# An adaLN transformer block on one core: a first modulation group of two k-tiles, an earlier silu(c) and x, and partition sums as matmuls with ones

## The chip, the core and the metric

The kernel runs on one core of one Trainium2 chip. The metric is the device time of one execution in microseconds (us). The engines are TensorE (PE; its weight loads are listed as PEld), VectorE (DVE), ScalarE (ACT), GpSimd (POOL) and SyncE (SP), which issues most DMAs. Each works through its own list of instructions in order.

## What is computed

One transformer block on 256 tokens with model width 2048, all in float32. A conditioning vector c gives six vectors of width 2048, which shift, scale and gate the two halves of the block:

```python
mod = silu(c) @ w_ada + b_ada
shift_m, scale_m, gate_m, shift_f, scale_f, gate_f = split(mod, 6)
h = modulate(rms_norm(x, pre_norm_mix), shift_m, scale_m)   # h * (1 + scale) + shift
q_n, k_c, v_c, k_s, v_s, k_w, v_w, g_n, q_m, k_m, v_m = split(h @ w_in)
o = concat(nsa_mixer(...), moba_mixer(...)) @ w_o
x = x + gate_m * rms_norm(o, post_norm_mix)
h = modulate(rms_norm(x, pre_norm_ffn), shift_f, scale_f)
x = x + gate_f * rms_norm(square(relu(h @ w_up)) @ w_down, post_norm_ffn)
```

w_ada is 2048 x 12288, w_in 2048 x 5656, w_up 2048 x 8192 and w_down 8192 x 2048. Every weight is read once.

## The kernel before

**Tiles.** The 256 tokens are two token tiles of 128; the width of 2048 is 16 k-tiles of 128. A product of float32 operands is made of three matmuls: both operands are split into a rounded high part and a low part, and `products` (L495) issues hi x hi (L496), hi x lo (L497) and lo x hi (L498). So each tile of weights needs an ACT cast for the high part (L491) and a DVE subtraction for the low part (L492) before PE can use it.

**The modulation vectors** are sums over 2048 rows of w_ada, with silu(c) as coefficients. They are not made on PE: `gemv_units` (L280) loads rows of w_ada and DVE multiplies each k-tile by its column of silu(c) (`csil`) and adds it to an accumulator of 128 partitions (L305 for the first, L310 for the others). What is left is a sum over the partitions: `reduce` (L338) transposes the accumulator on PE (L345), sums it up along the free axis on DVE (L347), and lets POOL add the bias (L351) and multiply by the norm gain (L353). Then `main` of `mod_units` (L356) scales and shifts the transposed, normalized x on ACT (L372), and splits it (L375 on ACT, L376 on DVE).

**Groups and passes.** M_MODS = (4, 4, 4, 4) says that the first half's modulation is made for four k-tiles at a time; the groups are named modm0, modm4, modm8 and modm12. The in-projection follows in passes: all six blocks of columns (kv, kw, qn, qm, km, vm; 1024 columns each, kw 536) for k-tiles 0 to 3, then all for 4 to 7, then qm and km for 8 to 11, and so on. Within a block the k-tiles are summed up in four PSUM banks. At the end of a block ACT copies the banks out in the first pass (L571), and in every later pass DVE adds them to what is there (L573). In F_MODS the second half's groups are modf0 to modf12.

**Order.** The program is a list of units (a load, a preparation, a main part), which `Stream.run` (L104) writes out in order. Loads run ahead as far as five raw buffers reach, preparations up to four units (AHEAD) and five split weight tiles (WBUFS). `spread` (L134) sets where in a pass the units of the next modulation group stand (L935 to L945): the group modm4 is made during the pass over k-tiles 0 to 3, and so on. A scheduler then settles the order on each engine; what stands under `tc.high_priority()` it brings forward. All large loads go through SP's queue.

**The start.** The six small DMAs of constants are on ACT's queue (L213 to L218); POOL builds an identity and the attention masks; the loads of modm0 begin, x follows (`x_units`, L513), is squared and summed on ACT (L525), scaled on DVE (L529) and transposed on PE (L274). In-projection products begin once modm0 has been summed up, and its k-tiles are modulated and split.

Of the kernel before, what the change touches and what calls it, by code (L numbers as in the profile page):

```python
# [12 lines left out]
F32 = mybir.dt.float32  # L13
F32R = mybir.dt.float32r
# [61 lines left out]
class Stream:  # L76
    """Emits units in order; loads and preparations run ahead as far as the buffers reach."""
# [56 lines left out]
def spread(base, extra, first, last):  # L134
    """The units of base with the groups in extra placed between positions first and last."""
# [17 lines left out]
def tile_adaln_block(ctx: ExitStack, tc: tile.TileContext, x, c, w_ada, b_ada, g_pm, g_qm, w_in,  # L153
# [28 lines left out]
    # Constants  # L182
    ident = cp.tile([P, P], F32, name="ident")
    make_identity(nc, ident)
    onesr = cp.tile([P, P], F32R, name="onesr")
    nc.scalar.activation(onesr, ident, AF.Identity, bias=1.0, scale=0.0)
    identb = cp.tile([P, P], BF16, name="identb")
    nc.vector.tensor_copy(identb, ident)
    sel4 = cp.tile([P, 32], F32, name="sel4")
    nc.vector.tensor_add(sel4, ident[:, 0:32], ident[:, 32:64])  # L190
    nc.vector.tensor_add(sel4, sel4, ident[:, 64:96])
    nc.vector.tensor_add(sel4, sel4, ident[:, 96:128])
    mhalf = cp.tile([P, 1], F32, name="mhalf")
    nc.gpsimd.memset(mhalf, -0.5)

    maskf = accp.tile([P, NT, NCMP + T], F32, tag="acc", name="maskf")
    nc.gpsimd.memset(maskf, 0.0)
    for t in range(NT):
        nc.gpsimd.affine_select(
            out=maskf[:, t, 0:NCMP], in_=maskf[:, t, 0:NCMP], compare_op=ALU.is_ge, fill=NEG,  # L200
            base=t * P - (CLEN - 1), pattern=[[-CSTR, NCMP]], channel_multiplier=1)
        nc.gpsimd.affine_select(
            out=maskf[:, t, NCMP:], in_=maskf[:, t, NCMP:], compare_op=ALU.is_ge, fill=NEG,
            base=t * P, pattern=[[-1, T]], channel_multiplier=1)
# [1055 lines left out]
```

## Time and profile before

| | |
|---|---|
| time, median of 3 runs | 1200.63 us (1200.17 to 1202.42) |
| span of the profiled execution, first to last instruction | 1199.2 us |
| PE busy | 1140.5 us, 95% |
| DVE busy | 908.5 us, 76% |
| ACT busy | 602.2 us, 50% |
| POOL busy | 32.7 us, 3% |
| mean DMA rate | 260 GB/s |

The page has no time of its own for the profiled execution but its span; the median of the runs is 1.4 us above it. Busy time is the time in which an instruction of the engine was running. A table of stretches gives, for each stretch of the span, the busy time of every engine with the number of instructions in parentheses, the granted clock of TensorE as a share of 2.4 GHz, the busy share of the DMA engines and the rate.

### The profile page before, as it was taken

What the parts mean: (1) busy time and instruction counts of PE and PEld (TensorE: products, weight loads), DVE (VectorE), ACT (ScalarE), POOL (GpSimd) and SP (SyncE); (2) the same over time, 40 slices, a digit from 0 to 9 for tenths busy, and PEclk for the clock granted to TensorE, in tenths of its full rate; (3) what the DMA queues carried; (4) which work ended last, traced back from release to release, by engine and by line L of the source; (5) the groups of instructions that cost most, each with busy time, mean ns of one, the idle gap of its engine ahead of it and who ended that gap; (6) DMA issues with size and microseconds to landing.
All of it is one profiled execution on the core that took longest, in us unless ns stands there. A gap on an engine that the chain in (4) does not pass through costs nothing.

```text
span 1199.2 us, 14451 instructions
## 1 busy us (share of the span) xinstructions
PE 1140.5 (95%) x5429; PEld 935.9 (78%) x5429; DVE 908.5 (76%) x1086; ACT 602.2 (50%) x922; POOL 32.7 (3%) x38
## 2 busy tenths in 40 slices
PE   2599998999999999999999999999999999999997
PEld 1477886878778887888888788888888888888885
DVE  6877999879998897876988986757666666665564
ACT  3446343436756666665343344767544444444441
POOL 1000001000000031000000000000000000000000
PEclk9699999999999999999999999999999999999999
DMA  9898989886766695997867875555677767775541
GB/s 334 311 392 277 361 307 336 261 293 246 273 223 233 246 356 178 360 333 276 315 250 279 315 266 193 176 176 187 215 258 268 259 253 274 253 278 178 207 142 70
DMA packets 88249, 312.02 MB, mean 260 GB/s; under 512 B 6051, under 2 KB 6515, under 8 KB 75251
## 3 DMA queue, kind: packets, MB, share of 16 engines
q1 hardware_dynamic: 87876, 311.01, 72.6%
q8 instruction: 42, 0.69, 0.2%
q14 instruction: 27, 0.21, 0.0%
q10 hardware_dynamic: 304, 0.11, 0.0%
HBM read 308.99 MB, written 2.10 MB: 259 GB/s over the span
## 4 chain that ended last, share of the span: by engine, by line
PE 81%; DVE 9%; issue 3%; DMA 3%; ACT 2%; POOL 1%; DVEq 0%; POOLq 0%; ACTq 0%
PE dps L498 9%; PE dps L496 9%; PE dps L497 9%; PE up L496 9%; PE up L498 9%; PE up L497 9%; DVE modm L310 3%; PE wo L496 2%; PE wo L498 2%; PE wo L497 2%; PE ft L1083 1%; PE in_vm L497 1%; PE in_vm L498 1%; PE in_vm L496 1%; PE in_kv L496 1%
## 5 line engine op out<-in xcount | busy, mean ns | idle before, releaser
L310 DVE SCALAR_TENSOR_TENSOR modf<-modf,csil,modf 128x1024 f32<-128x1024 f32 x60 | 76.7, 1278 | 9.2 <-DMA modf<-in_w_ada_dram 9.1
L310 DVE SCALAR_TENSOR_TENSOR modm<-modm,csil,modm 128x1024 f32<-128x1024 f32 x60 | 76.8, 1280 | 0.9
L1099 DVE TENSOR_TENSOR facc<-up,facc 128x512 f32<-128x512 f32 x96 | 61.5, 683 | 18.7 <-PE up L498 18.7
L310 DVE SCALAR_TENSOR_TENSOR gatef<-gatef,csil,gatef 128x1024 f32<-128x1024 f32 x32 | 40.6, 1278 | 1.3 <-DMA gatef<-in_w_ada_dram 1.3
L310 DVE SCALAR_TENSOR_TENSOR gatem<-gatem,csil,gatem 128x1024 f32<-128x1024 f32 x32 | 40.2, 1273 | 0.0
L1139 DVE TENSOR_TENSOR flo<-facc,fhi 128x512 fp32r<-128x512 f32 x32 | 21.7, 684 | 2.0 <-ACT fhi L1138 2.0
L1138 ACT CAST fhi<-facc 128x512 fp32r<-128x512 f32 x32 | 19.7, 624 | 5.3 <-PE up L497 1.9
L1101 ACT ACTIVATE facc<-facc 128x512 f32<-128x512 f32 x32 | 18.4, 624 | 2.8 <-DVE facc L1099 2.8
L1097 ACT COPY facc<-up 128x512 f32<-128x512 f32 x32 | 17.8, 594 | 1.6 <-PE up L498 1.0
L492 DVE TENSOR_TENSOR up_13lo<-up,up_13hi 128x1024 fp32r<-128x1024 f32 x8 | 9.8, 1226 | 11.5 <-ACT up_13hi L491 11.5
L492 DVE TENSOR_TENSOR up_14lo<-up,up_14hi 128x1024 fp32r<-128x1024 f32 x8 | 9.8, 1224 | 11.1 <-ACT up_14hi L491 11.1
L345 PE MATMUL modm0t<-ident,modm 128*128 128x128 f32 x8 | 1.9, 424 | 17.0 <-DVE modm L310 17.0
L1088 ACT ACTIVATE facc<-ft 128x512 f32<-128x512 f32 x32 | 17.2, 588 | 0.4 <-PE ft L1083 0.2
L1083 PE MATMUL ft<-ident,facc 128*128 128x128 f32 x128 | 16.8, 273 | 0.0
L1083 PEld LDWEIGHTS ft<-ident,facc 128*128 128x128 f32 x128 | 14.7, 140 | 2.6 <-ACT facc L1088 0.5
L492 DVE TENSOR_TENSOR up_0lo<-up,up_0hi 128x1024 fp32r<-128x1024 f32 x8 | 9.8, 1223 | 7.7 <-ACT up_0hi L491 7.7
L491 ACT CAST up_7hi<-up 128x1024 fp32r<-128x1024 f32 x8 | 8.4, 1056 | 14.3 <-PE up L498 14.3
L491 ACT CAST up_11hi<-up 128x1024 fp32r<-128x1024 f32 x8 | 8.4, 1055 | 14.2 <-PE up L498 14.2
L351 POOL TENSOR_TENSOR modf0red<-modf0red,cola 128x8 f32<-128x8 f32 x1 | 9.0, 8993 | 227.3 <-ACT wo_15hi L491 227.3
L491 ACT CAST up_10hi<-up 128x1024 fp32r<-128x1024 f32 x8 | 8.4, 1056 | 13.3 <-PE up L498 13.3
L491 ACT CAST up_6hi<-up 128x1024 fp32r<-128x1024 f32 x8 | 8.4, 1055 | 13.3 <-PE up L498 13.3
L345 PEld LDWEIGHTS modm0t<-ident,modm 128*128 128x128 f32 x8 | 1.6, 224 | 17.2 <-ACT in_kv_1hi L491 17.2
(2340 smaller groups left out, 4020.2 us busy)
## 6 DMA issues: line engine op xcount, KB each, us to landing
up<-in_w_up_dram SPq DMA_DIRECT2D x64, 1024.0 KB, 6.6
dn<-in_w_down_dram SPq DMA_DIRECT2D x64, 1024.0 KB, 4.9
modm<-in_w_ada_dram SPq DMA_DIRECT2D x64, 512.0 KB, 6.5
modf<-in_w_ada_dram SPq DMA_DIRECT2D x64, 512.0 KB, 5.9
gatem<-in_w_ada_dram SPq DMA_DIRECT2D x16, 1024.0 KB, 4.9
wo<-in_w_o_dram SPq DMA_DIRECT2D x16, 1024.0 KB, 5.3
gatef<-in_w_ada_dram SPq DMA_DIRECT2D x16, 1024.0 KB, 4.8
in_kv<-in_w_in_dram SPq DMA_DIRECT2D x8, 1024.0 KB, 7.3
```

Of the source, the lines that this page charges most:

```text
L310: nc.vector.scalar_tensor_tensor(part, w[:, j:j + step], csil[:, k:k + 1], part, ALU.mult, ALU.add)
L491: nc.scalar.copy(hi[:, 0:n], src)
L492: nc.vector.tensor_sub(lo[:, 0:n], src, hi[:, 0:n].bitcast(F32))
L496: nc.tensor.matmul(o, shi, whi, start=first, stop=False)
L497: nc.tensor.matmul(o, shi, wlo, start=False, stop=False)
L498: nc.tensor.matmul(o, slo, whi, start=False, stop=last)
L1083: nc.tensor.transpose(b[:, (2 * i + t) * P:(2 * i + t + 1) * P], f[:, t, (2 * j + i) * P:(2 * j + i + 1) * P], ident)
L1097: nc.scalar.copy(dst, b)
L1099: nc.vector.tensor_add(dst, b, dst)
L1101: nc.scalar.activation(dst, dst, AF.Relu)
L1138: nc.scalar.copy(hi, f)
L1139: nc.vector.tensor_sub(lo, f, hi.bitcast(F32))
```

## The change

- The first half's modulation is made in groups of 2, 2, 4, 4 and 4 k-tiles; the in-projection gets a pass over k-tiles 0 and 1 and a pass over k-tiles 2 and 3 in place of the one over 0 to 3. A group of two k-tiles is loaded four k-tiles of w_ada at a time (four DMAs of 256 KB each), where a group of four takes two at a time (two DMAs of 512 KB).
- The positions at which the units of the groups stand in the passes are new.
- silu(c) is computed at the start with high priority, straight from PSUM; the DMAs of x get high priority too, so that they stand ahead of those of w_ada. Masks, two identities, `sel4` and the positions' transposes move from the start into `late_constants`, in the pass over k-tiles 2 and 3; two small DMAs move from ACT's queue to SP's.
- `reduce` sums over the partitions with matmuls: each 128 x 128 piece of the accumulator is the stationary operand and a column of ones the moving one, so that one PSUM column per piece is the result. Bias and gain are applied by DVE.
- In the first group, odd k-tiles are modulated on DVE.

```diff
-M_MODS = (4, 4, 4, 4)
+M_MODS = (2, 2, 4, 4, 4)
...
+    one = cp.tile([P, 1], F32, name="one")
+    nc.gpsimd.memset(one, 1.0)
...
+    with tc.high_priority():
+        pc = bank("pconst0")
+        nc.tensor.transpose(pc[:, 0:16], stagec, ident[0:16, 0:16])
+        sigmoid_parts(csil, pc[:, 0:KD])
+        nc.vector.reciprocal(csil, csil)
+        nc.vector.tensor_mul(csil, csil, pc[:, 0:KD])
...
     def late_constants():
         nc.sync.dma_start(rp, rope)
         nc.sync.dma_start(w2[:, 0, :], ck_w2[0])
         nc.sync.dma_start(w2[:, 1, :], cv_w2[0])
+        nc.sync.dma_start(stageb[0:32, :], ck_pos[0])
+        nc.sync.dma_start(stageb[32:64, :], cv_pos[0])
+        nc.scalar.activation(onesr, ident, AF.Identity, bias=1.0, scale=0.0)
+        nc.scalar.copy(identb, ident)
+        mask_constants()
+        nc.vector.tensor_add(sel4, ident[:, 0:32], ident[:, 32:64])
+        nc.vector.tensor_add(sel4, sel4, ident[:, 64:96])
+        nc.vector.tensor_add(sel4, sel4, ident[:, 96:128])
+        pb = bank("pconst")
+        nc.tensor.transpose(pb[:, 0:64], stageb, ident[0:64, 0:64])
+        nc.scalar.copy(colb, pb[:, 0:64])
...
-        units = gemv_units(name, base + k0 * P, W, True, 2 if W <= 512 else 1, acc, first)
+        units = gemv_units(name, base + k0 * P, W, True, min(1024 // W, 4), acc, first)
...
-                for i0 in range(0, 2 * nk, 4):
-                    n = min(4, 2 * nk - i0)
-                    b = bank(f"{name}t{i0}")
-                    for i in range(n):
-                        nc.tensor.transpose(b[:, i * P:(i + 1) * P],
-                                            acc.t[:, (i0 + i) * P:(i0 + i + 1) * P], ident)
-                    nc.vector.tensor_reduce(red[:, i0:i0 + n],
-                                            b[:, 0:n * P].rearrange("p (k q) -> p k q", k=n),
-                                            axis=AX.X, op=ALU.add)
+                b = bank(f"{name}t")
+                for i in range(2 * nk):
+                    nc.tensor.matmul(b[:, i:i + 1], acc.t[:, i * P:(i + 1) * P], one,
+                                     start=True, stop=True)
                 ks = slice(k0, k0 + nk)
-                nc.gpsimd.tensor_add(red.rearrange("p (s k) -> p s k", s=2),
-                                     red.rearrange("p (s k) -> p s k", s=2), bias[:, :, ks])
-                nc.gpsimd.tensor_mul(red[:, nk:], red[:, nk:], gcol[:, ks])
+                nc.vector.tensor_add(red.rearrange("p (s k) -> p s k", s=2),
+                                     b[:, 0:2 * nk].rearrange("p (s k) -> p s k", s=2),
+                                     bias[:, :, ks])
+                nc.vector.tensor_mul(red[:, nk:], red[:, nk:], gcol[:, ks])
...
-                    modulate(xv[:, k % 2, :], xv[:, k % 2, :], *of(k))
+                    if tag == "m" and k0 == 0 and k % 2:
+                        shift, scale = of(k)
+                        nc.vector.tensor_scalar(xv[:, k % 2, :], xv[:, k % 2, :], scale, shift,
+                                                ALU.mult, ALU.add)
+                    else:
+                        modulate(xv[:, k % 2, :], xv[:, k % 2, :], *of(k))
...
-            for h, v in enumerate(st["x"]):
-                nc.sync.dma_start(v, x[t * P:(t + 1) * P, h * 1024:(h + 1) * 1024])
+            with tc.high_priority():
+                for h, v in enumerate(st["x"]):
+                    nc.sync.dma_start(v, x[t * P:(t + 1) * P, h * 1024:(h + 1) * 1024])
...
-    base = flat(in_pass(blocks, 0, 4))
-    m0 = [u for grp in mods[0] for u in grp]
-    stream.add(m0[:8] + [early(u) for u in base[:2]] + m0[8:])
-    base += [Unit(None, late_constants)]
-    stream.add(spread(base, mods[1], 6, len(base) - 7))
+    base = flat(in_pass(blocks, 0, 2))
+    m0 = flat(mods[0])
+    stream.add(m0[:3] + [early(base[0])] + m0[3:])
+    stream.add(spread(base, mods[1], 1, len(base) - 3))
+    base = flat(in_pass(blocks, 2, 4))
+    base.insert(2, Unit(None, late_constants))
+    stream.add(spread(base, mods[2], 0, len(base) - 2))
     base = flat(in_pass(blocks, 4, 8))
-    stream.add(spread(base, mods[2], 2, len(base) - 5))
+    stream.add(spread(base, mods[3], 0, len(base) - 5))
...
-    stream.add(spread(base, mods[3][:-1], 0, len(base)))
-    stream.add(mods[3][-1])
+    stream.add(spread(base, mods[4][:-1], 0, len(base)))
+    stream.add(mods[4][-1])
```

## Rows read from the trace of the kernel before

**Rows 1.** The page: busy us of each engine, share of span, instructions.

```profile
PE 1140.5 (95%) x5429; PEld 935.9 (78%) x5429; DVE 908.5 (76%) x1086; ACT 602.2 (50%) x922; POOL 32.7 (3%) x38
```

**Rows 2.** Stretches: us, busy of PE, PEld, DVE, ACT, POOL, PEclk, DMA share, GB/s.

```profile
15.00:37.30 22.30, 5.07 (x31) 4.36 (x29) 21.36 (x20) 6.88 (x18) 1.59 (x1) 0.72 1.04 393
37.30:112.80 75.50, 66.67 (x305) 54.41 (x306) 58.35 (x56) 41.59 (x61) 4.27 (x4) 0.92 0.88 323
112.80:175.60 62.80, 61.76 (x297) 51.43 (x296) 58.66 (x66) 26.70 (x32) 2.18 (x2) 1.00 0.90 325
175.60:200.70 25.10, 22.04 (x93) 16.91 (x92) 24.99 (x25) 6.57 (x7) 0.00 (x0) 1.00 0.96 357
200.70:226.40 25.70, 24.20 (x110) 19.52 (x109) 21.26 (x26) 11.02 (x16) 4.01 (x3) 1.00 0.74 253
...
500.00:780.00 280.00, 279.42 (x1261) 231.43 (x1260) 223.48 (x235) 139.91 (x168) 2.97 (x7) 1.00 0.76 271
```

**Rows 3.** Chain that ended last, 0 to 45: start us, us, what.

```profile
4.98 4.73 DMA x<-in_x_dram
...
37.42 1.96 PE modm0t L345 x8
39.39 0.70 DVE modm0red L347
...
41.35 1.07 POOL modm0red L353
42.45 1.58 ACT xnm L372 x3
...
44.59 0.79 PE in_kv L496
```

**Rows 4.** Timeline of DVE: start us, us, engine, line, operation, count.

```profile
12.49 0.16 DVE L260 TENSOR_REDUCE xr<-xss 128x1 f32<-128x2 f32 x1 [0.80 <-ACT xj L525]
14.98 0.74 DVE L305 TENSOR_SCALAR modm<-modm,csil 128x1024 f32<-128x1024 f32 x1
...
199.13 1.28 DVE L310 SCALAR_TENSOR_TENSOR modm<-modm,csil,modm 128x1024 f32<-128x1024 f32 x1
```

**Rows 5.** Groups of DVE instructions, 112.8 to 200.8: busy, mean ns, idle before.

```profile
L310 DVE SCALAR_TENSOR_TENSOR modm<-modm,csil,modm 128x1024 f32<-128x1024 f32 x28 | 35.8, 1277 | 0.2
L573 DVE TENSOR_TENSOR qm<-in_qm,qm 128x512 f32<-128x512 f32 x8 | 5.2, 680 | 0.0
L573 DVE TENSOR_TENSOR wide<-in_kw,wide 128x268 f32<-128x268 f32 x4 | 1.5, 425 | 0.0
L376 DVE TENSOR_TENSOR modm8lo<-xnm,modm8hi 128x512 fp32r<-128x512 f32 x2 | 1.4, 694 | 1.7 <-ACT modm8hi L375 1.6
L492 DVE TENSOR_TENSOR in_km_6lo<-in_km,in_km_6hi 128x1024 fp32r<-128x1024 f32 x1 | 1.2, 1228 | 0.0
```

**Rows 6.** Stretches, columns as in rows 2; and SP's issue of w1k.

```profile
32.00:37.00 5.00, 0.00 (x0) 0.00 (x0) 4.87 (x4) 1.77 (x2) 0.00 (x0) 0.50 1.03 408
...
233.00:236.00 3.00, 3.00 (x27) 3.00 (x26) 2.93 (x6) 2.19 (x3) 0.00 (x0) 1.00 0.99 285
...
230.17 4.85 SPq L654 DMA_DIRECT2D w1k<-in_cmp_k_w_dram  x2
```

**Rows 7.** Timelines of PE around a reduction's transposes and a small float32 matmul.

```profile
86.53 1.03 PE L345 MATMUL modm4t<-ident,modm 128*128 128x128 f32 x8
87.32 0.48 PE L498 MATMUL in_qm<-in_qm_3hi,modm0lo 128*128 128x512 f32 x1
...
255.31 0.40 PE L497 MATMUL in_qn<-in_qn_12lo,modm12hi 128*128 128x512 f32 x1
255.54 0.30 PE L679 MATMUL chidk<-sel,cpartk 128*128 128x32 f32 x2
255.68 0.48 PE L498 MATMUL in_qn<-in_qn_12hi,modm12lo 128*128 128x512 f32 x1
```

**Rows 8.** Stretch with the fall of the granted clock, columns as in rows 2.

```profile
24.00:28.00 4.00, 0.00 (x0) 0.00 (x0) 3.89 (x4) 0.00 (x0) 0.00 (x0) 0.61 1.05 388
```

More of the change, by code (lines that the diff above doesn't have):

```diff
@@ L180, in rawtile, with sigmoid_parts @@
         return wp.tile([P, 2048], F32, tag="raw", bufs=RAWBUFS, name=name)
+    def sigmoid_parts(dst, src):
+        nc.vector.tensor_scalar(dst, src, -87.0, None, ALU.max)
+        nc.scalar.activation(dst, dst, AF.Exp, scale=-1.0)
+        nc.vector.tensor_scalar(dst, dst, 1.0, None, ALU.add)
     ident = cp.tile([P, P], F32, name="ident")
     make_identity(nc, ident)
[L185 to L192, printed above, removed]
     mhalf = cp.tile([P, 1], F32, name="mhalf")
     nc.gpsimd.memset(mhalf, -0.5)
[L196 to L204, printed above, removed]
-    mask = cp.tile([P, NT, NCMP + T], BF16, name="mask")
-    nc.vector.tensor_copy(mask, maskf)
-    rp = cp.tile([P, NT, 2, HD], F32, name="rp")
+    one = cp.tile([P, 1], F32, name="one")
+    nc.gpsimd.memset(one, 1.0)
+    cola = cp.tile([P, P], F32, name="cola")
+    colb = cp.tile([P, 64], F32, name="colb")
+    csil = cp.tile([P, KD], F32, name="csil")
     stagea = accp.tile([P, P], F32, tag="acc", name="stagea")
@@ L216, in tile_adaln_block, with columns, mask_constants @@
     nc.scalar.dma_start(stagea[112:128, :], g_pf.rearrange("b (r p) -> (b r) p", p=P))
-    nc.scalar.dma_start(stageb[0:32, :], ck_pos[0])
-    nc.scalar.dma_start(stageb[32:64, :], cv_pos[0])
-    w2 = cp.tile([P, 2, HD], F32, name="w2")
+    with tc.high_priority():
[4 more added lines that the diff above has]
+        nc.vector.tensor_mul(csil, csil, pc[:, 0:KD])
+    def columns():
+        pa = bank("pconst2")
+        nc.tensor.transpose(pa[:, 0:P], stagea, ident)
+        nc.vector.tensor_copy(cola, pa[:, 0:P])
+        for i in (1, 4):
+            scale = cola[:, i * KD:(i + 1) * KD]
+            nc.vector.tensor_scalar(scale, scale, 1.0, None, ALU.add)
+    onesr = cp.tile([P, P], F32R, name="onesr")
+    identb = cp.tile([P, P], BF16, name="identb")
+    sel4 = cp.tile([P, 32], F32, name="sel4")
+    mask = cp.tile([P, NT, NCMP + T], BF16, name="mask")
+    rp = cp.tile([P, NT, 2, HD], F32, name="rp")
+    w2 = cp.tile([P, 2, HD], F32, name="w2")
+    def mask_constants():
+        maskf = accp.tile([P, NT, NCMP + T], F32, tag="acc", name="maskf")
+        nc.gpsimd.memset(maskf, 0.0)
+        for t in range(NT):
+            nc.gpsimd.affine_select(
+                out=maskf[:, t, 0:NCMP], in_=maskf[:, t, 0:NCMP], compare_op=ALU.is_ge, fill=NEG,
+                base=t * P - (CLEN - 1), pattern=[[-CSTR, NCMP]], channel_multiplier=1)
+            nc.gpsimd.affine_select(
+                out=maskf[:, t, NCMP:], in_=maskf[:, t, NCMP:], compare_op=ALU.is_ge, fill=NEG,
+                base=t * P, pattern=[[-1, T]], channel_multiplier=1)
+        nc.scalar.copy(mask, maskf)
     def late_constants():
@@ L908, in tile_adaln_block @@
     mods = [mod_units("m", k0, n, xnm, hstat) for k0, n in zip(k0s, M_MODS)]
-    stream.add([x_units(0), x_units(1)])
+    xu = [x_units(0), x_units(1)]
+    columns()
+    stream.add(xu)
     gm = gate_units("m", g_qm, gate_m)
```

24 lines of the change are left out of this document (1 added, 23 removed).

## The prediction

> **What bounds the kernel now.** I began with the page's engine line [rows 1]: PE is busy for 95% of the span, DVE for 76%. By that line alone, anything that lets PE begin earlier is gained in full. So I read the chain of waits next, from the start to PE's first product [rows 3]. The reader is to see that PE is held up by another engine here: x lands 4.73 us after its issue at 4.98, DVE works through modm0, PE transposes what is left, DVE, POOL and ACT follow one after the other, and the first in-projection product stands at 44.59. Then the stretches [rows 2], which show that the share of 76% is a mean over unlike stages. From 112.8 to 175.6 (the second pass) PE is busy for 61.8 of 62.8 us, but DVE is busy for 58.7; from 175.6 to 200.7 DVE is busy for 25.0 of 25.1 us and PE for only 22.0. From 500 on PE is busy for 279.4 of 280 us, and DVE has room. So up to 200, DVE is as much the bound as PE. DVE has slack in the first pass alone: 58.4 busy of 75.5 us between 37.3 and 112.8. The question for this change is DVE's total up to its last accumulation of the last group, L310 at 199.13, which ends at 200.4 [rows 4].
>
> **PE's head start.** x is issued at about 0.74 (the place of the first load now) instead of 4.98 [rows 3], so DVE's first step on x moves from 12.49 to 12.49 - 4.24 = 8.25 [rows 4]. Up to the end of the first group, DVE then has the 2.5 us that lie between 12.49 and 14.98 [rows 4], about 1.7 us for the second half of x (an estimate, less than those 2.5 us took for the first half and csil), 16 accumulations of 512 columns instead of 1024, at about 0.66 each (10.6), and one weight split, 1.2 [rows 5]: it ends near 24.2. The loads wanted by then are x 2.1 MB, modm0 4.2 MB and a block of weights 1.05 MB, 7.3 MB; at 393 GB/s [rows 2] that is 18.7 us, and with a start-up of some 2.7 us they land near 21.4, just ahead of DVE. The chain behind was 44.59 - 37.42 = 7.2 us [rows 3]. It loses one of two reductions per group and POOL's two steps (2.4 us between DVE's end at 40.1 and ACT's start at 42.45), and one of two modulations goes beside the other onto DVE; what stays is a PE sum (at most the 1.96 us of the transposes), two short DVE steps and about 1.1 us of ACT (half of the 2.14 us from 42.45 to 44.59, in which four steps ran). I take 3.3. First product: 27.5, so PE begins 17 us earlier.
>
> **What that meets on DVE.** A pass over two k-tiles has half the PE work, 61.8 / 2 = 31 us [rows 2]. The pass over k-tiles 2 and 3 is a later pass, so DVE adds its 24 banks (20 of 512 columns, 4 of 268) where ACT had copied the first pass's. It also makes modm4 (15 x 1.28 + 0.74 = 19.9 us) and ten splits of 1.2 and two of half the width, about 0.7 (13.4) [rows 4, 5]. With the adds, 14.5 us, that is 48 us of DVE against 31 of PE: the head start runs dry in this pass, and PE waits for DVE from there to 200.
>
> So I sum up DVE. From 15.0 to 200.7 it was busy for 21.36 + 58.35 + 58.66 + 24.99 = 163.4 us and idle for 22.3 [rows 2]. The change gives it:
> - 20 x 0.65 + 1.5 = 14.5 us of adds (8 took 5.2 of busy time, the four of kw 1.5) [rows 5];
> - minus three groups' reductions, 2 x 0.70 each [rows 3]: -4.2;
> - plus a bias and a gain step in each of four groups. No row shows such a small step on PSUM; bounds are 0.16 (a step on one column [rows 4]) and 0.43 (268 columns from PSUM [rows 5]). I take 0.16, the nearer size: 8 x 0.16 = 1.3, with 3.4 as the upper end;
> - 2.5 us between 12.49 and 14.98 that are inside the count now [rows 4];
> - two half-width accumulations in place of one, 16 times: 512 columns took 0.68 as an add [rows 5], twice that is 1.36 against 1.28, so about +1.0;
> - `sel4` and one modulation on DVE, at most 0.68 a step [rows 5] and mostly far less: 0.8.
>
> Together 179.3 us, begun at 8.25: without any idle time DVE would end at 187.6 instead of 200.4. So 12.8 us is the most that can be gained up to there, and each us of DVE's idle time takes one away. I allow for 9: 2.5 in the first chain, 1.7 in each of three later ones (the wait for ACT's high part in modm8 [rows 5]), and 1.5 for loads in the pass over k-tiles 0 and 1. Ends: 3 (as tight as after 175.6) and 14 (two thirds of before's 22.3). Gain up to 200: 12.8 - 9 = 3.8 us, between -1.2 and 9.8.
>
> **Behind 200.** From 200.7 to 226.4 PE is idle for 1.5 us [rows 2]. The last group's shorter chain gives back part: -1.0 (ends 0 and -1.5). After that PE is the bound, and what was gained stays.
>
> **The sums as matmuls.** Eight transposes held the products up by 87.32 - 86.53 = 0.79 us. Two small float32 matmul instructions, which is what one float32 matmul becomes there, made the step from one product to the next 0.37 us instead of 279.42 / 1261 = 0.22, so 0.07 each [rows 2, 7]. Sixteen of them cost 1.2 (2.4 by their busy time of 0.30 for two): 0.4 us more in each group of four. In the first half DVE covers this. In the second half's four groups PE has no slack: +1.6 us, ends 0 and 6. There the freed reductions and POOL steps are worth nothing, since PE is busy for 279.4 of 280 us.
>
> **Edits at nothing.** Masks, identities and constants in `late_constants` are wanted only by attention; ACT (26.7 of 62.8 us busy in the second pass) and POOL (2.2) cover them [rows 2]. Without that cover they would cost some 3 us. Two more small DMAs on SP stand ahead of weights loaded ahead of need. The copy-outs that ACT loses were not on the path.
>
> **Rows of 1 KB.** Groups of two load w_ada in pieces of 256 columns, 1 KB, where before it was 2 KB. No row shows 1 KB. With 2 KB and more, 408 GB/s were moved between 32 and 37; with the 512-byte rows of w1k, issued from 230.2 on, 285 GB/s at a DMA share of 0.99 [rows 6]. So modm0's 4.2 MB take between 10.3 and 14.7 us: 0 to 4.4 us more at the start. I take 0.5, nearer to the row that is a bound by bytes, and inside the 9 us of idle time. The Trainium skill's page "DMA: Bandwidth & Descriptors", section Specifications, says that transfers of 512 bytes and more run at line rate; by it this term is 0. The 285 GB/s row speaks against it at 512 bytes.
>
> **Sum.** -3.8 - 1.0 + 1.6 = -3.2 us on the profiled span of 1199.2, so 1196.0. The runs' median lies 1.4 us above the span: **1197.4 us**, 0.3% faster. This case's own range follows from the idle time, 3 to 11.5 us (beyond that it is the third rival's): 1191.4 to 1199.9.
>
> **Rivals.**
> - **The head start is kept.** DVE has next to no idle time: 12.8 + 1.0 - 1.6 = 12.2 gained, 1188.4. For it: DVE is idle for only 0.1 us from 175.6 to 200.7, so it can run without gaps [rows 2]. Against it: modm0's chain and the loads of the first pass leave gaps that no order fills.
> - **DVE does not count.** If PE alone set the time, its 17 us would come through whole, less the 1.6 of the sums: 1200.6 - 15.4 = 1185.2. For it: PE is busy for 95% of the span [rows 1]. Against it: the stretches up to 200.7, and DVE's sum [rows 2]. The Trainium skill's page "Perfetto Trace Analysis", section Identifying the Most-Contended Engine, has the most contended engine optimized first, and judges TensorE by the share of its weight loads; at 78% against DVE's 76% that is PE here too, and by this rule over the whole span the time would be this rival's.
> - **The extra pass eats all.** DVE's idle time is 13 us or more (static order, preparations only four units ahead): 1200 to 1202, no change. For it: DVE was idle for 17 us of the first pass before [rows 2]. A slow 1 KB load of 4.4 us ends here too.
> - **PE goes slow, and the kernel gets slower.** Place: the pass over k-tiles 2 and 3, where PE has 31 us of work in DVE's 48. Before, PE had nothing to do after x's transposes, and the granted clock fell, to a mean of 0.61 from 24 to 28 and 0.50 from 32 to 37 [rows 6, 8]. If that happens in this pass, 31 us of products take 62 at 1.2 GHz instead of 2.4, 14 more than DVE's 48: 1197.4 + 14, less some 4 of DVE's idle time that this would cover, is about 1207. It decides as soon as slices of that pass show a granted clock under 1.00 for most of its length. Against it: from 175.6 to 200.7 PE was idle for 3 of 25 us in pieces, and the clock stayed at 1.00 [rows 2].
> - **No such effect at all:** if PE's first product does not come earlier, because csil or w_ada wait behind x, DVE still gets some 13 us more work than it loses; less some 8 us that the first pass's idle time of 17 would take up, 1200.6 + 5 = about 1205. The sum of loads speaks against it.
>
> **How the numbers follow.** Forecast 0.48, kept head start 0.18, DVE does not count 0.04, eaten 0.20, slow clock 0.06, no earlier start 0.04. The range leaves out the last two, the second rival and the tails: 1187.5 to 1201.5. A measurement of this kernel can tell about 0.2%, 2.4 us, from no change: faster is below 1198.2. That is all of the two cases with more head start and 0.38 of the forecast's 0.48 (6.8 of the 8.5 us of its range): 0.60. Slower (above 1203) is 0.10, the two last cases; the rest, 0.30, is within.
>
> **What the profile would show.** Right: first in-projection product near 27.5; DVE busy for 95% or more from 45 to 195; PE idle for more than 10 us in pieces in the pass over k-tiles 2 and 3; the last L310 of the first half's groups near 196; nothing changed from 500 on but about 0.4 us a group. Wrong: PE without gaps in that pass (then DVE's sum is too large, and the gain nearer to 12); DVE with gaps of several us there, or granted clock under 1.00; modm0's loads landing after 24, which would be the 1 KB rows.

## The result, and the profile after

The changed kernel takes **1214.72 us** (median of 4 runs, 1212.7 to 1216.03), against 1200.59 of the kernel before beside it: a ratio of 1.011, with an interval of 1.0095 to 1.0126. It is slower by some 14 us, where 1197.4 was predicted, and outside the range of 1187.5 to 1201.5. The profiled execution took 1212.7 us and has a span of 1210.9.

The page's engine line after the change, against [rows 1]:

```profile
PE 1154.7 (95%) x5493; PEld 946.8 (78%) x5493; DVE 915.8 (76%) x1128; ACT 602.3 (50%) x921; POOL 13.3 (1%) x23
```

PE has 64 instructions and 14.2 us of busy time more. The shares of PE, DVE and ACT are the same to a per cent, so this line does not show where the 14 us lie. The stretches do. They are cut at the same events as [rows 2], shifted to where these events are now: 33.0 is the first in-projection product, 69.1 and 114.8 are the ends of the passes over k-tiles 0 and 1 and over 2 and 3, 183.0 is the end of the pass over 4 to 7. Columns are us, busy time of PE, PEld, DVE, ACT and POOL, then PEclk, DMA share and GB/s.

```profile
15.00:33.00 18.00, 3.69 (x24) 3.29 (x23) 15.51 (x24) 5.91 (x15) 1.54 (x3) 0.67 1.08 360
33.00:69.10 36.10, 34.58 (x152) 27.95 (x153) 27.90 (x33) 23.72 (x38) 0.00 (x0) 0.93 0.89 315
69.10:114.80 45.70, 37.04 (x162) 28.18 (x162) 42.74 (x52) 17.47 (x24) 0.00 (x0) 0.96 0.89 321
114.80:183.00 68.20, 65.32 (x305) 53.75 (x305) 64.70 (x75) 25.93 (x30) 0.00 (x0) 0.97 0.89 320
183.00:205.80 22.80, 21.58 (x93) 17.02 (x92) 22.69 (x23) 6.01 (x6) 0.00 (x0) 1.00 0.96 356
205.80:231.80 26.00, 25.68 (x124) 21.28 (x124) 19.43 (x25) 12.08 (x17) 1.81 (x1) 1.00 0.65 215
500.00:780.00 280.00, 280.00 (x1272) 232.53 (x1271) 220.33 (x232) 136.71 (x163) 1.81 (x1) 1.00 0.77 273
```

The early start did come: the first product stands at 33.0 where it was at 44.6. But the passes over k-tiles 0 to 3, which ended at 112.8 before, end at 114.8, and the next pass at 183.0 instead of 175.6. The head start is gone by 110, and the kernel is late from there on. How late it is at seven points is read from the timeline of PE (start of the first product of each block and k-tile, changed minus before, in us). At the start of up the products stand in another order in the two kernels, so the start of the 73rd one is taken there; the 72 ahead of it are the same.

| start of | before | changed minus before |
|---|---|---|
| in_kv_0 | 44.59 | -11.57 |
| in_kv_4 (second pass of before) | 112.77 | +2.08 |
| in_kv_11 | 212.77 | +4.64 |
| wo_10 | 426.77 | +5.58 |
| wo_12 (behind the first FFN sum) | 433.11 | +6.53 |
| 73rd product of up (behind the residual and its norm) | 489.95 | +9.24 |
| up_12 | 738.45 | +11.22 |

So two losses stand apart. One lies in the first half, 16 us from in_kv_0 to in_kv_11, of which 11.6 is the head start itself. The other begins at wo_10, where the passes are the same as before and only the sum differs: 3.7 us up to the 73rd product of up, and 2.0 more up to up_12, with three more sums of the FFN between. That was the clue: this second part sits at a step that I had priced at 0.4 us a group.

### The profile page after: what moved, and what is told of

Its sections match the earlier page's. It is cut to its first block, busy times and chain, and to the rows that moved or that the text cites. A ratio compares the mean times of both kernels' runs of the same rounds, so it can differ in the third digit from the quotient of the medians.

```text
span 1210.9 us, 14618 instructions
## 1 busy us (share of the span) xinstructions
PE 1154.7 (95%) x5493; PEld 946.8 (78%) x5493; DVE 915.8 (76%) x1128; ACT 602.3 (50%) x921; POOL 13.3 (1%) x23
## 4 chain that ended last, share of the span: by engine, by line
PE 82%; DVE 10%; issue 3%; DMA 2%; ACT 2%; POOL 0%; DVEq 0%; SPq 0%; POOLq 0%; ACTq 0%
PE dps L505 10%; PE dps L503 10%; PE dps L504 10%; PE up L505 9%; PE up L503 9%; PE up L504 9%; DVE modm L315 3%; PE wo L503 2%; PE wo L504 2%; PE wo L505 2%; PE ft L1095 1%; DMA wo<-in_w_o_dram 1%; PE in_qm L504 1%; PE in_qn L503 1%; PE in_qn L504 1%
## 5 line engine op out<-in xcount | busy, mean ns | idle before, releaser
L315 DVE SCALAR_TENSOR_TENSOR modm<-modm,csil,modm 128x1024 f32<-128x1024 f32 (+1 forms) x75 | 80.2, 1070 | 1.0
L504 PE MATMUL up<-up_1lo,xmhi 128*128 128x512 f32 x32 | 12.7, 395 | 2.5 <-DVE up_1lo L499 2.5
L498 ACT CAST up_9hi<-up 128x1024 fp32r<-128x1024 f32 x8 | 8.4, 1056 | 13.2 <-DVE up_8lo L499 8.3
L498 ACT CAST up_14hi<-up 128x1024 fp32r<-128x1024 f32 x8 | 8.4, 1050 | 12.6 <-PE up L505 12.6
L498 ACT CAST up_5hi<-up 128x1024 fp32r<-128x1024 f32 x8 | 8.4, 1056 | 12.4 <-PE up L505 9.1
L498 ACT CAST up_8hi<-up 128x1024 fp32r<-128x1024 f32 x8 | 8.4, 1055 | 11.7 <-PE up L505 11.7
L498 ACT CAST up_7hi<-up 128x1024 fp32r<-128x1024 f32 x8 | 8.4, 1053 | 11.6 <-PE up L505 11.6
```

Of the source, the lines that this page charges most:

```text
L315: nc.vector.scalar_tensor_tensor(part, w[:, j:j + step], csil[:, k:k + 1], part, ALU.mult, ALU.add)
L498: nc.scalar.copy(hi[:, 0:n], src)
L504: nc.tensor.matmul(o, shi, wlo, start=False, stop=False)
```

## The experiments

Two theories came first. Theory A had two separate losses, one in the passes, one from the sums; theory B let the sums off and had the passes do it all. Ratios are to the kernel before, which was run again beside each set of runs. Its medians there lie between 1200.6 and 1201.7 us, so a difference between the times of two sets can be off by some 1 us.

**The sums alone, and the sums undone.** In the kernel before:

```diff
-  nc.tensor.transpose(b[:, i*P:(i+1)*P], acc.t[:, (i0+i)*P:(i0+i+1)*P], ident)   # then tensor_reduce of the bank
+  nc.tensor.matmul(b[:, i:i+1], acc.t[:, i*P:(i+1)*P], one, start=True, stop=True)
-  nc.gpsimd.tensor_add(red, red, bias); nc.gpsimd.tensor_mul(red[:, nk:], ..., gcol)
+  nc.vector.tensor_add(red, b, bias);   nc.vector.tensor_mul(red[:, nk:], ..., gcol)
```

> The kernel before with one part of the change: all eight groups are summed by 128x1 matmuls with ones, and bias and gain go to VectorE; the groups, the passes and the start stay. Theory A (two separate losses, the second from the sums: the first FFN group's sum takes PE 0.95 us more, and the order in which ACT and VectorE take up the residual and the norm behind the output projection gets worse by some 4.7 us, the rest of the FFN adds 0.4): 1206 to 1208 us. Theory B (the middle of the kernel loses its time because the stream comes to it otherwise after the new passes, not by the sums): 1201 to 1203 us, which is 16 matmuls and a cold start more.

Measured: 1212.59 us, 1.0102 (1.0084 to 1.012). That is above both theories: the sums alone make nearly the whole loss, about twice what theory A gave them.

The same edit backwards in the changed kernel:

> The changed kernel with the sums of all groups as before (transposes, a VectorE reduce of the bank, bias and gain on POOL). Theory A: the losses behind 430 us go away, the 5.4 us that the passes lose stay: 1206 to 1209 us. Theory B: the sums are worth 2 us at most: 1212 to 1215 us.

Measured: 1204.3 us, 1.0034 (1.0021 to 1.0047), 1.7 us under theory A. The passes and the start keep 3.7 us of loss; undoing the sums, POOL's steps with them, gives 10.4 back.

And backwards for the four FFN groups only (`if tag == "m"` new, else old):

> The changed kernel with the sums of the four FFN groups alone as before; the five groups of the mixer keep the matmuls with ones. Theory A: nearly all of what the sums cost lies behind 430 us, so 1207 to 1210 us, within 2 us of the kernel with all sums as before. Theory B: 1212 to 1215 us.

Measured: 1207.57 us, 1.0062 (1.0047 to 1.0077), theory A's time, but 3.3 us from the kernel with all the old sums, where it allowed 2. So 7.1 of these 10.4 us lie in the FFN groups, and 3.3 in the mixer's.

**The passes of before in the changed kernel.** `M_MODS = (4, 4, 4, 4)` and the order of units of before; early start and new sums stay.

> The changed kernel with mixer groups of four k-tiles and the passes of before (k-tiles 0 to 3, 4 to 7, and so on): silu(c) and x still come first and the sums are still matmuls. Theory A (the pass more costs the head start and 5 us besides, by VectorE's 22 more additions and splits that come late, with a slow TensorE clock behind the waits): the first in-projection product comes at 38 to 41 us and the first half ends level with before or up to 5 us ahead of it; with the sums' 6 us behind 430 us that is 1202 to 1207 us. Theory B (the first half loses by the early start itself, constants and x on ACT and SP ahead of their old place): 1210 us or more.

Measured: 1213.47 us, 1.011 (1.0095 to 1.0125). By its letter this is theory B's number, but for another reason: it differs from the kernel with the sums alone by 0.9 us, less than either's spread. The first half is not spoiled by the early start; the sums cost more than theory A had put down.

**Order or matmuls?** What can a sum of 1.7 us on PE cost beyond itself? ACT's timeline around the second group in the kernel with the sums alone (start us, us, engine, line, operation, count, and in brackets the idle time before it and what ended it):

```profile
89.62 0.59 ACT L569 COPY qm<-in_qm 128x512 f32<-128x512 f32 x1 [1.89 <-PE in_qm L496]
90.11 1.58 ACT L370 ACTIVATE xnm<-xnm,modm4red 128x256 f32<-128x256 f32 x3
91.60 0.60 ACT L373 CAST modm4hi<-xnm 128x512 fp32r<-128x512 f32 x1
92.10 0.60 ACT L370 ACTIVATE xnm<-xnm,modm4red 128x256 f32<-128x256 f32 x1
92.61 1.03 ACT L489 CAST in_km_0hi<-in_km 128x1024 fp32r<-128x1024 f32 x1
```

and the same place in the kernel before:

```profile
87.00 1.06 ACT L491 CAST in_km_0hi<-in_km 128x1024 fp32r<-128x1024 f32 x1
87.95 1.06 ACT L491 CAST in_km_1hi<-in_km 128x1024 fp32r<-128x1024 f32 x1
90.82 1.59 ACT L372 ACTIVATE xnm<-xnm,modm4red 128x256 f32<-128x256 f32 x3 [1.80 <-POOL modm4red L353]
```

The reader is to see the order. Before, ACT cast the high parts of in_km_0 and in_km_1 while the sum was under way, and modulated then. Now the modulation stands ahead of these casts in ACT's list, and ahead of it the copy of a finished bank. The copy waits 1.89 us for a product that PE runs behind the sum, the modulation follows, and the cast of in_km_0 comes at 92.61 instead of 87.00. PE waits for it, and in_km_0 starts 5.35 us late:

```profile
93.69 0.97 PE L494 MATMUL in_km<-in_km_0hi,modm0hi 128*128 128x512 f32 x3 [2.71 <-ACT in_km_0hi L489]
```

Nobody wrote this order: a scheduler settles each engine's list when the program is built, and the edit to the sums moved what stands around them. Why it came out so (perhaps a sum without reduces and POOL steps counts as shorter) is not shown.

To put the order back without the transposes, two VectorE instructions of 512 columns on the dead accumulator were put behind each sum, as long as the reduces had been, and bias and gain back on POOL:

```diff
+  for j in range(2): nc.vector.scalar_tensor_tensor(v_j, v_j, b[:, j:j+1], v_j, ALU.mult, ALU.add)   # v_j: 512 columns of acc.t
```

> The kernel before with the sums as 128x1 matmuls with ones, bias and gain on POOL as before, and behind each sum two VectorE instructions of 512 columns on the accumulator that is no longer needed (work that the result does not use), about as long as the two reduces of before. That puts ACT's list of the first half back: the casts of the next weight tiles stand ahead of the modulation again; around the residual behind the output projection the list stays as with the plain sums. Theory A (the order of ACT's list is what costs, not the matmuls): in_km_0's first product comes within 1.5 us of the kernel before (it was 5.3 us late with the plain sums), the first half ends 0 to 2 us late instead of 4 to 5, the loss behind 430 us stays: 1206 to 1209 us. Theory B (the matmuls themselves, or what they leave of PE's clock, cost): 1212 us or more, and in_km_0 is late by 4 us or more.

Measured: 1213.86 us, 1.0101 (1.0086 to 1.0116). The number is theory B's, yet the trace does not decide for it. The casts came ahead of the modulation as meant, but one copy more of a finished bank stood ahead of both: at 90.46 ACT waits 1.63 us for PE's products behind the sum, with in_km_0's cast behind it, and in_km_0 starts 3.7 us late, between the two theories. The list was not the one of before, and the run says only that a longer chain does not help. It is inconclusive.

**Bias and gain alone.** Transposes and reduces as before, only POOL's two steps on VectorE:

```diff
-  nc.gpsimd.tensor_add(...); nc.gpsimd.tensor_mul(...)
+  nc.vector.tensor_add(...); nc.vector.tensor_mul(...)
```

> The kernel before with bias and gain on VectorE instead of POOL; the sums stay transposes and VectorE reduces. ACT's and VectorE's lists stay nearly as they were. Theory A (the order follows the length of the sum with its reduces, not where bias and gain run): 1199 to 1202 us. Theory B (the modulation that is ready earlier, by the POOL instructions that fall away, is what disturbs the splits): 1204 us or more.

Measured: 1196.39 us, 0.9955 (0.994 to 0.997): 2.6 us under theory A's lower end, a gain that neither theory had. The rows of modm4's small tile, in the kernel before and in this one (duration in ns, least, median and greatest; first and last start):

```profile
L351 POOL TENSOR_TENSOR modm4red<-modm4red,cola x1: 1111/1111/1111, 88.5 to 88.5; 128x8 f32<-128x8 f32 x1
L353 POOL TENSOR_TENSOR modm4red<-modm4red,cola x1: 1059/1059/1059, 89.7 to 89.7; 128x4 f32<-128x4 f32 x1
```

```profile
L351 DVE TENSOR_TENSOR modm4red<-modm4red,cola x1: 163/163/163, 88.7 to 88.7; 128x8 f32<-128x8 f32 x1
L353 DVE TENSOR_TENSOR modm4red<-modm4red,cola x1: 159/159/159, 89.9 to 89.9; 128x4 f32<-128x4 f32 x1
```

Eight numbers a partition took POOL 1.1 us and VectorE 0.16. By PE's starts the gain is made at the groups of the first half: -2.8 us at in_kv_4, -5.6 at in_kv_11, and no more behind it. ACT's list moved here too: at modm4, modm8 and modm12 casts of the next weight tiles now stand ahead of the modulation, so how much of the gain is the shorter chain alone is not shown. What the matmuls with ones cost has to be counted from this kernel: 1212.59 - 1196.39 = **16.2 us** (17.4 by the starts of up_12 in the two profiles).

**One instruction for a sum instead of two.** A float32 matmul becomes two instructions here, so a group of four has 16. With fp32r operands it is one; the weights are a constant of ones and the moving operand is a copy of two columns of the accumulator, so the sums themselves are left out; bias and gain are on VectorE:

```diff
-  nc.tensor.matmul(b[:, i:i+1], acc.t[:, i*P:(i+1)*P], one, ...)
+  nc.vector.tensor_copy(tiny, acc.t[:, 0:2])                       # tiny: 128x2, fp32r
+  nc.tensor.matmul(b[:, 2*i:2*i+2], onesr, tiny, ...)
```

> The kernel before with the new sums, each as one TensorE instruction instead of two: fp32r operands, a constant matrix of ones as weights and two columns that VectorE copies from the accumulator, so the sums themselves are left out and the modulation takes wrong values, while the instructions wait for the same accumulator. The lists of ACT and VectorE are nearly those of the kernel with the new sums alone. A sum of four k-tiles takes TensorE 8 instructions instead of 16, about 0.85 us instead of 1.70 us. Theory A (the second instruction per sum is what TensorE pays, 0.9 us in each of seven or eight groups, and the order of the lists costs the rest): 1204 to 1208 us, with 3 us or more of loss left in the first half and behind the output projection. Theory B (TensorE's time in the sums is all): 1196 to 1201 us, since bias and gain on VectorE alone gave 1196.4 us. Theory C (the order is all): 1210 us or more.

Measured: 1201.0 us, 1.0 (0.999 to 1.0009): at theory B's upper edge, 3 us under theory A. So the second instructions are most of it, and the trace shows what is left. PE's timeline around the second sum, in the kernel with the new sums and in this one:

```profile
87.40 1.84 PE L345 MATMUL modm4t<-one,modm 128*128 128x1 f32 x16
89.10 0.49 PE L496 MATMUL in_qm<-in_qm_3hi,modm0lo 128*128 128x512 f32 x1
```

```profile
85.04 0.95 PE L347 MATMUL modm4t<-modm4tiny,onesr 128*128 128x2 f32 x8
85.86 0.47 PE L496 MATMUL in_qm<-in_qm_3hi,modm0hi 128*128 128x512 f32 x1
```

From the start of the sum to the next product it is 89.10 - 87.40 = 1.70 us for 16 and 85.86 - 85.04 = 0.82 for 8; the eight transposes took 0.79 [rows 7]. All are 0.10 to 0.106 us an instruction, with 1, 2 or 128 columns moved: the count is the price, not the columns. And ACT's list is another by one line here (over the whole kernel the two lists differ in only one place more, at a cast of up_11 in the FFN):

```profile
85.73 1.05 ACT L491 CAST in_km_0hi<-in_km 128x1024 fp32r<-128x1024 f32 x1
86.67 1.59 ACT L372 ACTIVATE xnm<-xnm,modm4red 128x256 f32<-128x256 f32 x3
```

The cast is ahead of the modulation again, and the loss at in_km_0 is gone. PE's starts, each against the kernel before:

| start of | bias and gain alone | one instruction a sum | new sums alone |
|---|---|---|---|
| in_kv_0 | -1.06 | -1.57 | +0.25 |
| in_km_3 | -2.78 | -2.05 | +4.93 |
| in_kv_11 | -5.56 | -4.61 | +4.09 |
| wo_12 | -5.77 | -4.80 | +5.32 |
| 73rd product of up | -5.82 | -0.78 | +8.99 |
| up_12 | -5.32 | -0.33 | +12.08 |

The 16.2 us come apart here. The last two columns differ by 12.4 at up_12. The first sum runs at a granted clock of 0.50, where 16 instructions took 3.7 us and 8 took 2.0 (VectorE's wait for them); with what follows it makes 2.6 us by in_kv_1. Seven later groups times 1.70 - 0.82 = 0.88 are 6.2. That is 8.8 us for the second instructions themselves. The step from in_kv_1 to in_km_3 makes 4.4, of which 0.9 are the sum. The other 3.5 lie at the cast behind the modulation: PE's wait of 2.7 us for it (0.8 for the parts of in_km_1 in the kernel with one instruction), and the clock behind that wait. With the new sums alone:

```profile
94.00:96.00 2.00, 1.71 (x6) 1.05 (x5) 2.00 (x3) 2.00 (x4) 0.00 (x0) 0.72 0.00 0
96.00:98.00 2.00, 2.00 (x6) 1.61 (x5) 1.77 (x3) 2.00 (x5) 0.00 (x0) 0.50 0.14 15
```

With one instruction a sum the granted clock is 1.00 from 86 to 94. What the first two columns differ by, 5.0 at up_12, is not the count, which is 8 in both. Of it 4.1 arise between wo_12 (1.0) and the 73rd product of up (5.0). PE's waits from 425 to 490 (us in total, times, longest), in the kernel before, in this one and in the changed one:

```profile
PE x2t L1045 <- issue: 1.4, 2, 1.1
PE up L497 <- DVE up_1lo L492: 0.5, 1, 0.5
PE up L496 <- ACT xmhi L375: 0.4, 1, 0.4
```

```profile
PE up L497 <- DVE up_1lo L492: 2.5, 1, 2.5
PE up L496 <- ACT xmhi L375: 1.2, 1, 1.2
```

```profile
PE up L504 <- DVE up_1lo L499: 2.5, 1, 2.5
PE up L503 <- ACT xmhi L382: 1.3, 1, 1.3
```

The same two waits, to a tenth, with 8 or 16 instructions a sum, and not without the new sums. ACT's timeline shows the list behind the longer one, first in the kernel before, then in the changed one:

```profile
473.26 1.10 ACT L491 CAST up_1hi<-up 128x1024 fp32r<-128x1024 f32 x1
474.47 0.64 ACT L1033 ACTIVATE xa<-x 128x512 f32<-128x512 f32 x1
```

```profile
479.72 0.63 ACT L1045 ACTIVATE xa<-x 128x512 f32<-128x512 f32 x1 [0.35 <-DVE x L1043]
...
483.12 1.07 ACT L498 CAST up_1hi<-up 128x1024 fp32r<-128x1024 f32 x1
```

The cast that PE's product waits for, through VectorE's low part, stood ahead of the four squares of the residual and stands behind them now. That is order again. (With 8 instructions a sum PE also ran at a granted clock of 0.50 from 474 to 476, behind the wait of 2.5 us; in the changed kernel the clock is 1.00 there. So the 4.1 us are not these waits alone.) Of what the sums cost, then, about 9 us are the matmuls' own, by the run with half the instructions. About 8 go with the lists: they are read from these waits and the clock behind them, since no run has put the old lists back around the new sums.

**The start and the passes.** With the old sums in place the rest of the change can be taken apart. The early start alone (groups of four, passes and sums of before):

> The kernel before with silu(c) and x first and late constants as changed, and nothing else: groups of four, passes, sums, bias and gain on POOL as before. Theory A (the early start alone is worth 1 to 3 us): 1198 to 1200 us. Theory B (it is lost in the first passes): 1200 to 1203 us. With it the passes alone are priced: the changed kernel with the old sums took 1204.3 us.

Measured: 1199.88 us, 0.9991 (0.9981 to 1.0), theory A, at its edge. So the passes cost 1204.3 - 1199.9 = 4.4 us. With bias and gain on VectorE in both:

> The changed kernel with transposes and VectorE reduces for the sums as before, and bias and gain on VectorE as changed: all of the change but the matmuls with ones. Theory A (the parts add up: bias and gain on VectorE gain 5.3 us on the old passes, the passes lose 3.7 us): 1197 to 1201 us. Theory B (with the passes of two k-tiles the chain behind a sum is hidden by other waits, and nothing is gained from a shorter one): 1203 to 1206 us.

Measured: 1200.38 us, 0.9998 (0.9989 to 1.0007), theory A.

> The kernel before with silu(c) and x first and late constants as changed, bias and gain on VectorE, but groups of four k-tiles, the passes of before and the old sums. The lists of ACT and VectorE behind the first half are those of the kernel before with bias and gain on VectorE alone, which took 1196.4 us. Theory A (the early start is worth what it gives the first sum, some 2 us, and VectorE carries it through): 1193 to 1196 us. Theory B (it is lost on the way, as the 2.4 us were in the kernel with four-tile groups and new sums): 1196 to 1199 us.

Measured: 1195.98 us, 0.9958 (0.9943 to 0.9973), on the border of the two theories. The passes cost 1200.4 - 1196.0 = 4.4 us here too, and bias and gain on VectorE are worth 3.9 us with either passes. In the changed kernel the matmuls with ones cost 1214.7 - 1200.4 = 14.3 us, and the parts add up: -0.9 + 4.4 - 3.9 + 14.3 = 13.9 us, where 14.1 were measured.

Why do passes over two k-tiles lose 4.4 us with PE 10 to 13 us ahead at their start? The first theory was the sum of VectorE's work. So the additions of the extra pass were cut to 8 columns each (the other columns of that pass are left out of the result):

```diff
-  nc.vector.tensor_add(dst, b[:, 0:wd], dst)
+  n = 8 if g == 2 else wd                                # g: first k-tile of the pass
+  nc.vector.tensor_add(dst[:, 0:n], b[:, 0:n], dst[:, 0:n])
```

> The changed kernel with the old sums, and in the pass over k-tiles 2 and 3 each VectorE addition takes 8 columns instead of 512 (268 for kw): the other columns of that pass's products are left out of the result. It costs VectorE some 14 us less (24 additions at about 0.68 and 0.43 us against about 0.1 each). Theory A (VectorE's work sets the pace up to its last accumulation, so the additions of the extra pass ate the head start): the time falls by 6 to 13 us against the same kernel with the additions, to 1191 to 1198 us. Theory B (TensorE's slow stretches, the smaller DMA rows or late splits ate it, whatever VectorE's sum is): it falls by under 4 us, 1200 us or more.

Measured: 1201.62 us, 1.0002 (0.9988 to 1.0017), 2.7 us less (3.8 by the ratios): theory B. VectorE was busy for 64.0 of 77.0 us from 33 to 110, before its additions were cut for 71.5 of 82.2 up to 115.2; the work that went became idle time in part. By PE's starts in the two profiles the additions weigh more where they stand than in the time: without them in_kv_4 comes 5.5 us earlier and in_kv_11 4.0, but up_12 only 0.4. (This kernel's ten runs lie between 1198.2 and 1205.1 us, the profiled one at 1204.9.)

Then half of the additions were saved by letting three blocks go over k-tiles 0 to 3 in one pass:

```diff
-  flat(in_pass(blocks, 0, 2)) ... flat(in_pass(blocks, 2, 4))
+  flat(in_pass(blocks[:3], 0, 2)) ... flat(in_pass(blocks[:3], 2, 4) + in_pass(blocks[3:], 0, 4))
```

> The changed kernel with the old sums, and the pass of its own over k-tiles 0 and 1 for three of the six blocks alone (kv, kw, qn); the other three (qm, km, vm) go over k-tiles 0 to 3 in one pass, so that 12 of 24 additions, 8.2 us of VectorE, fall away, while TensorE has 13.7 us of products instead of 30 before k-tiles 2 and 3 have to be there. Theory A (VectorE's sum counts): 1196 to 1201 us, at or below the kernel before. Theory B (other causes): within 2 us of the changed kernel with the old sums, 1202 to 1206 us.

Measured: 1202.59 us, 1.0011 (1.0001 to 1.0021), 1.7 us less (2.8 by the ratios): theory B by its time, between the two by the ratios.

The second theory was PE's clock. The stretches around two waits of PE, in the changed kernel with sums as before and bias and gain on VectorE (columns as above):

```profile
88.00:90.00 2.00, 0.00 (x0) 0.00 (x0) 2.00 (x3) 0.00 (x0) 0.00 (x0) 1.00 1.02 412
90.00:92.00 2.00, 1.57 (x4) 1.29 (x5) 2.00 (x3) 1.96 (x2) 0.00 (x0) 0.66 1.02 394
92.00:94.00 2.00, 2.00 (x6) 1.54 (x6) 1.90 (x2) 1.08 (x2) 0.00 (x0) 0.50 0.91 304
134.00:136.00 2.00, 1.63 (x5) 1.35 (x6) 2.00 (x4) 0.05 (x1) 0.00 (x0) 0.75 1.01 400
136.00:138.00 2.00, 2.00 (x6) 1.52 (x6) 2.00 (x4) 0.00 (x0) 0.00 (x0) 0.50 1.04 395
```

PE waited 3.6 us for in_qm_2lo up to 90.4, and when it went on, it ran at 1.2 GHz for some 3.5 us. Ahead of 134.4 it waited 1.3 and 0.6 us, and ran at 1.2 GHz from 135 to 138. Each slow stretch costs PE about half of its length. So PE was given something to do in these waits, products into a bank that nothing reads:

```diff
+  FILL = {('in_qn2', 3): 14, ('in_qn4', 4): 6}
+  for _ in range(n): nc.tensor.matmul(b, shi, whi[:, 0:512], start=True, stop=True)   # behind that block's k-tile
```

> All of the change but the matmuls with ones (sums by transposes and reduces, bias and gain on VectorE), with TensorE kept busy ahead of its two long waits in the first half: 14 products of 512 columns into a bank that nothing reads behind block qn in the pass over k-tiles 2 and 3 (about 3.2 us, where it waited 3.6 us), and 6 behind in_qn_4 in the pass over k-tiles 4 to 7 (about 1.4 us, where it waited 1.3 us). Without them the granted clock was 0.50 to 0.66 at 90 to 94 us and 0.50 to 0.90 at 134 to 140 us, and products took 0.43 us apart instead of 0.23. Theory A (the slow clock behind these waits is most of what the passes lose): the clock stays at 1.00 there, and the time falls by 2 to 3.6 us from 1200.4 us, to 1197 to 1198.5 us. Theory B (VectorE's list sets the pace of these passes, TensorE being slow only fills waits that would come anyway): within 1 us of 1200.4 us, the clock at 1.00 or not. Theory C (the products come late to where they were to fill): 1201 us or more.

Measured: 1198.26 us, 0.9971 (0.9963 to 0.998): theory A. The same stretches now:

```profile
88.00:90.00 2.00, 2.00 (x10) 1.32 (x8) 2.00 (x4) 1.09 (x2) 0.00 (x0) 1.00 1.01 408
90.00:92.00 2.00, 2.00 (x9) 1.66 (x10) 2.00 (x2) 1.40 (x2) 0.00 (x0) 1.00 1.02 371
92.00:94.00 2.00, 2.00 (x12) 1.63 (x11) 2.00 (x4) 1.51 (x2) 0.00 (x0) 1.00 0.79 229
134.00:136.00 2.00, 2.00 (x10) 1.66 (x9) 2.00 (x4) 0.00 (x0) 0.00 (x0) 1.00 1.01 398
136.00:138.00 2.00, 2.00 (x10) 1.64 (x10) 2.00 (x2) 1.20 (x2) 0.00 (x0) 1.00 1.02 355
```

and a stretch ahead of them, where the kernel without these products had a granted clock of 1.00:

```profile
78.00:80.00 2.00, 1.77 (x5) 0.94 (x4) 2.00 (x5) 0.00 (x0) 0.00 (x0) 0.53 1.05 379
80.00:82.00 2.00, 2.00 (x6) 1.62 (x7) 2.00 (x2) 0.00 (x0) 0.00 (x0) 0.62 1.00 397
```

Products that nobody needs made the kernel 2.1 us faster (3.2 by the ratios). Two slow stretches went and one came in this profile, and the order of PE's products moved around in_qm_2 as well. So about half of the passes' 4.4 us goes with PE's waits and its slow clock behind them; that it is the clock alone is not shown. The same in the kernel with the early start, the passes and sums of before, and bias and gain on VectorE, ten transposes of a dead accumulator in the wait between the first sum and in_kv_0:

> The fastest so far (1196.0 us: passes and old sums of before, silu(c) and x first, bias and gain on VectorE) with ten transposes into a bank that nothing reads between the first sum and in_kv_0, where TensorE waits for the modulation and then runs its first k-tile at a granted clock of 0.50. Theory A (a TensorE that works through this wait has its clock back earlier, and the first k-tiles end earlier): 1194 to 1195.5 us. Theory B (VectorE's list sets the end of the first half anyway): 1195.5 to 1197 us.

Measured: 1194.97 us, 0.9956 (0.994 to 0.9972). By PE's starts the first half ends 2.4 us earlier than without them (in_kv_11 at -7.0 instead of -4.6), but the ratio is that of the kernel without them, and their intervals lie over each other. Whether it is faster is not settled; both beat both kernels.

## Why the prediction was wrong, point by point

- **What bounds the kernel.** Right that 95% of PE says little and that VectorE's list counts up to 200. Wrong in what followed: I treated lists as amounts of work, and about half of what the sums cost goes with their order.
- **PE's head start.** 27.5 was predicted, 33.02 measured. x was issued at 1.23, behind one load of w_ada, and VectorE's first step on it came at 9.16 (8.25 predicted). The first group's last accumulation ended at 28.6 instead of 24.2: the first one began 2.8 us behind that step (2.5 in the sum), an accumulation of 512 columns took 0.75 us, not 0.66, and two weight splits of 1.2 us stood ahead of the last ones, where the sum had one. The chain behind took 4.3 us instead of 3.3, of which the sum's 8 instructions, at a granted clock of 0.50, were 1.84.
- **VectorE's sum.** The amount was right, in part by luck: the half-width accumulations took 0.76 us each, so that term is 16 x (1.52 - 1.28) = 3.8 us by its own reckoning, and not 1.0. The idle time was not right. From its first step on x to the end of the last accumulation:

```profile
9.16:205.44 196.28, 165.39 (x748) 133.21 (x749) 178.10 (x218) 83.93 (x124) 4.43 (x7) 0.94 0.92 329
9.16:33.02 23.86, 7.23 (x41) 6.63 (x41) 20.45 (x40) 10.82 (x28) 4.43 (x7) 0.75 1.08 361
33.02:114.85 81.83, 71.67 (x313) 56.15 (x314) 70.67 (x84) 41.17 (x61) 0.00 (x0) 0.95 0.89 318
114.85:205.44 90.59, 86.49 (x396) 70.43 (x395) 86.99 (x96) 31.94 (x36) 0.00 (x0) 0.98 0.91 330
```

  VectorE was busy for 178.1 us (179.3 predicted) and idle for 18.2 (9 predicted, 14 at most), of which 11.2 lie in the passes over k-tiles 0 to 3. There VectorE waits for high parts from ACT and for PE's sums, ACT for banks from PE or for loads, and PE for low parts from VectorE. It is not the new sums: with the old ones VectorE was idle for 10.7 us from 33 to 115.2. Which link of this ring ends it is not settled; the runs show that the additions are worth 2.7 us in the time and the fill of PE's two waits 2.1, and these need not add up.
- **The sums as matmuls.** The step that failed most. Predicted +1.6 us in the second half and nothing in the first, where VectorE was to cover it; measured 16.2 in all on the passes of before and 14.3 in the changed kernel. Of the forecast's miss of 17.3 us, 12.7 lie here; the head start, the passes and the shorter chain were to give 4.8 and gave 0.4, which is the other 4.4. Of the price, 0.07 us an instruction came from a pair between two long products [rows 7]; in a row of 16 it is 0.106, so a group costs 0.9 and not 0.4. PE paid that in the first half too, at the first group at half its clock. The Trainium skill's page "TensorE: Matmul & The Clock Gate", section LDWEIGHTS (loading the stationary operand), gives the time of that load as the columns divided by 1.2, in ns, which is 107 ns for 128; by it an estimate of the sum is 16 x 0.107 = 1.71 us, and the trace agrees with 1.70 at a granted clock of 1.00. The other 8 us, a cast behind a copy and a modulation and a cast behind four squares, were in no term at all.
- **POOL's steps.** They were in the sum as part of the first chain and as -1.0 behind 200. In all groups together they were worth 3.9 to 5.3 us by the runs; in the kernel before, 1.1 of it was there at in_kv_0, 2.8 at in_kv_4 and 5.6 at in_kv_11, so the groups behind the first had such a chain on the path too.
- **Rows of 1 KB and edits at nothing.** 360 GB/s at a DMA share of 1.08 from 15 to 33, against 393 [rows 2]; modm0's loads were ahead of VectorE, and VectorE waited for none of them, so the term was 0 and not 0.5. The late constants cost nothing that a run shows: the early start with them gained 0.9 us.
- **Rivals.** "The extra pass eats all" (0.20) is what the passes do: 1200.38 and 1204.3 with the old sums, where it gave 1200 to 1202. "PE goes slow" (0.06) had the right mechanism at a smaller size: two stretches of some 3.5 us each, one in that pass and one in the next, and about 2 us, not 10. No rival had the sums as its mechanism, so no case reached 1214. The chance of 0.10 for slower was too small because the one part of the change that adds to the bound engine, in every group, had been given ends of 0 and 6 us in the second half, nothing in the first, and no rival.

## What to carry to other kernels

Where lists are ordered when the program is built, a step that is changed can move what stands around it in every list that waits for it; so look at what now stands behind the waiting instruction on its engine, and compare the lists before the times. Price small matmuls by their number (0.1 us each here at a granted clock of 1.00), not by their columns; a float32 one counts twice. Take a change of several parts apart before it is judged: this one held 4 to 5 us of gain (bias and gain on VectorE) under 14 to 16 us of loss.

## What the runs showed of the hardware that was not expected

- A TensorE instruction with a 128x128 float32 or fp32r stationary operand took 0.10 to 0.106 us in a row of its kind, with 1, 2 or 128 moving columns, and about 0.21 at a granted clock of 0.50.
- An elementwise step on 128x8 took POOL 1.06 to 1.11 us and VectorE 0.16.
- After waits of 3.6 us and of 1.3 and 0.6 us TensorE ran at a granted clock of 0.50 for some 3.5 us. With useless products in the waits the clock stayed at 1.00 there and fell once elsewhere, and the kernel went from 1200.4 to 1198.3 us.
